# A hybrid decoder step: second score product over all rows, no GpSimd at the feed forward's entry, output projection in two halves

## The chip, the cores and the metric

One core of a Trainium2 chip runs the whole program: one layer over 1024 prompt tokens and 32 decode tokens (8 sequences of 4). The metric is the device time of one execution in microseconds (us). Engines are named as in the profile: PE (TensorE, with PEld for its weight loads), DVE (VectorE), ACT (ScalarE), POOL (GpSimd), SP (SyncE, which only issues DMAs here).

## The reference, cut to what matters

```
h  = rmsnorm(x, rms1_g) * (1 + sc1) + sh1                      # adaLN per sequence
z  = h @ w_in + b_in          # q, k, v, forget logits, glu_a, glu_b, gate_a, gate_b
s  = q @ k.T / 8 + C_q - C_k, causal;  p = softmax(s);  o = p @ v     # C = cumsum(logf)
y_a = o @ w_pa                                                 # attention branch
y_b = silu(layernorm(depthwise_conv(glu))) @ w_pb + b_pb       # convolution branch
m  = sigmoid(gate_a) * y_a + sigmoid(gate_b) * y_b
x  = x + g1 * (m @ w_o)                                        # output projection
h2 = rmsnorm(x, rms2_g) * (1 + sc2) + sh2
f_gate, f_up = split(h2 @ w_ffn_in)                            # 1024 -> 2 * 2816
x  = x + g2 * ((silu(f_gate) * f_up) @ w_ffn_out)
y  = rmsnorm(x, final_g)
```

D_MODEL is 1024, there are 8 heads of 64, and everything is float32. The 32 decode tokens attend to 1024 cached positions each.

## The kernel before, in words

Features lie on the 128 partitions and tokens along the free axis: the T = 1056 tokens (1024 prompt, 32 decode) are columns, and the 1024 features are KD = 8 tiles. A float32 product is made of three float32r products: an operand is split into a high part (an ACT cast, `wh`, L312) and the rest (a subtraction on DVE or POOL, `wl`, L315), and high times high, high times low and low times high are added up in PSUM (`mm3`, L324 to L326). `split_ahead` runs such a split at high priority, ahead of its turn.

The stages, in order of the code: input projection and the convolution; decode attention; prompt attention (`softmax_rows`, `load_head`, `scores`, `weighted`), with gate products and adaLN products (`gate`, `ada`) between; the two branches (`branch`, once for the convolution and once for attention); the output projection with `w_o`; the feed forward; its second projection with the last norm.

*Prompt attention.* A unit is a head and a pair of 128-row blocks. For each block `softmax_rows` makes scores in pieces of up to 512 columns in one PSUM tile `pss`: a first product of `q` and `k` over 128 rows (L813; the 64 upper rows hold one part of the split q, the 64 lower ones the other, and k's high part is there twice), a mask for the last piece (L815), and a second product over the 64 rows of `sl` alone, high q with low k (L816). Then DVE takes a minimum (L818), ACT an exponential (L824). `weighted` turns the probabilities (L871) and multiplies them with v (L883, L884). `load_head` brings a head in by seven DMAs, of which one is `kl` (L848).

*Branches.* `branch` goes over 8 row tiles and, in each, over three pieces of CW3 = 352 tokens. `out_a`, of the attention branch, adds the two gated branches on POOL (L965) and splits the sum into 48 pieces of 16 `rows` tiles (L966, L967), which are the inputs `merged` of the output projection.

*Output projection.* Three blocks `c` of 352 tokens. Each block loads and splits all eight tiles of `w_o`, multiplies (24 matmuls of 352 columns per tile), adds the residual (`residual`, L1051) and sums squares (L1066); `rstd` then makes 1/rms of the block with small DVE operations (L200 to L211) and spreads it over the partitions by diagonal tiles `dg` and a product with ones (L216, L217), and ACT copies it into `R` (L1090). After block 1 stands `half_factors(0)`.

*Feed forward.* It runs in halves `q` of SUP = 528 tokens, each of two quarters of HS = 264, by Winograd's form of Strassen's scheme: `half_factors(q)` makes seven split sums of the normed input (`u` L1011 and L1013, differences L1030, L1033, L1035, L1040, splits L1019 and L1020), `pair_weights` seven split sums of the weights (L1124, L1125, sums L1134, L1136, L1137, L1139), and `hidden_half` seven products of 12 matmuls with 264 columns (L1167): 84 matmuls per tile and half. Tiles 0 to 3 run for half 0 alone at first, tiles 4 to 21 for both, and tiles 0 to 3 for half 1 at the end. POOL takes part: the differences L1030 and L1033, two of the seven splits of `half_factors`, the weight sums of tiles 1 to 3 (not 0, `DV`), and four splits of `w_o` in block 2.

A scheduler with its own estimate of durations orders each engine's instructions; they then run in that order. Tile pools set when a buffer is free again.

The lines that choose engine and width before:

```
w = split_ahead(w_o[j], KD, pool if c == 2 and j % 2 else dve, *where)
w = pair_weights(t, dve if len(halves) == 2 or t in DV else pool)
```

Of the kernel before, what the change touches and what calls it, by code (L numbers as in the profile page):

```python
# [48 lines left out]
DV = (0,)  # L49
# [38 lines left out]
def hybrid_step(ctx, tc, xT, cT, vec, bvf, con, stT, ptab, ptabr, kcT, vc, lfc, w_ada, w_in, w_vfa, w_vfb,  # L88
# [97 lines left out]
    def rstd(s, n, denom):  # L186

        nb = -(-n // P)
        nf = n // P
        v = sm.tile([P, 4], F32, name="rv", tag="rv", bufs=2)  # L190
# [13 lines left out]
        y = sm.tile([P, 4], F32, name="ry", tag="ry", bufs=2)[:, :nb]  # L204
        t = sm.tile([P, 4], F32, name="rt", tag="rt", bufs=2)[:, :nb]
# [7 lines left out]
        pr = ps_st()  # L213
        for b in range(nb):
            m = min(P, n - b * P)
            dve.tensor_scalar(dg[:m, b * P:b * P + m], ident[:m, :m], y[:m, b:b + 1], None, OP.mult)  # L216
            pe.matmul(pr[:, b * P:b * P + m], ones[:m, :], dg[:m, b * P:b * P + m], start=True, stop=True)  # L217
        return pr
# [615 lines left out]
    def load_head(h):  # L834
# [111 lines left out]
    def branch(which, src, w_p, out):  # L946
        xs = split_act(src)
        for j in range(KD):
            w = split_ahead(w_p[j], 4, pool)
            for o in range(0, T, CW3):  # L950
                zg = ev(wp, "gev", 4)[:, :CW3]
                sp.dma_start(zg, gD[which][j][:, o:o + CW3])
                act.activation(zg, zg, AF.Sigmoid)
                ps = ps_mm()
                gemm(ps, w, lambda k: (xs[k][0][:, o:o + CW3], xs[k][1][:, o:o + CW3]), 4, CW3)
                out(j, o, ps[:, :CW3], zg)
# [5 lines left out]
    def out_a(j, o, ps, zg):  # L962
        h, l = [merged(o // CW3, r, j) for r in range(2)]
        dve.tensor_tensor(zg, ps, zg, OP.mult)
        (pool if j < KD - 1 else dve).tensor_tensor(zg, zg, X(j)[:, o:o + CW3], OP.add)  # L965
# [3 lines left out]
    branch(1, cvD, w_pb, out_b)  # L969
# [6 lines left out]
    def bp_tile(i, dt=F32R):  # L976
        return bp.tile([P, 3 * CW3], dt, name="b", tag=f"b{i}", bufs=1)
# [3 lines left out]
    def merged(c, r, j):  # L981
        i = (c * 2 + r) * KD + j
        return rows[i // 3][:, i % 3 * CW3:(i % 3 + 1) * CW3]

    branch(0, oD, w_pa, out_a)
# [7 lines left out]
    def half_factors(q, new):  # L993
# [66 lines left out]
    def sq_add(s, first, x, n, eng=dve):  # L1060
        if first:
            act.activation(s[:, :n], x, AF.Square)
        else:
            q = ev(sm, "sq", 2, (P, 400))
            act.activation(q[:, :n], x, AF.Square)
            eng.tensor_tensor(s[:, :n], s[:, :n], q[:, :n], OP.add)  # L1066

    for c in range(3):
        o = CW3 * c
        s = sm.tile([P, 400], F32, name="s1", tag="ssum", bufs=2)  # L1070
        for j in range(KD):
# [9 lines left out]
            ps = ps_mm()  # L1081
            gemm(ps, w, lambda k: (merged(c, 0, k), merged(c, 1, k)), KD, CW3)
            xj = X(j)[:, o:o + CW3]
            with tc.high_priority() if j == KD - 1 else nullcontext():
                residual(xj, ps, j, o, CW3, 16, xr)
                sq_add(s, j == 0, xj, CW3)
            sp.dma_start(xD[:, j, o:o + CW3], xj)
        with tc.high_priority():
            pr = rstd(s, CW3, D)
        act.copy(R[:, o:o + CW3], pr[:, :CW3])  # L1090
        if c == 1:
# [36 lines left out]
    def pair_weights(t, eng):  # L1128
# [270 lines left out]
```

## Time and profile before

| | |
|---|---|
| runs shown | 1669.34, 1672.14, 1674.14 us; median 1672.14 |
| profiled execution | 1673.01 us, its span 1671.2 us |
| PE busy | 1600.6 us, 96% of the span, 10988 matmuls |
| DVE, ACT, POOL busy | 1074.1 us (64%), 702.6 us (42%), 251.9 us (15%) |
| granted clock, mean | 0.98 of full speed |
| moved by DMA | 263.93 MB, mean 158 GB/s |

The span is what lies between the first and the last instruction of the trace; 1.8 us lie around it. PE is the busiest engine nearly everywhere, but its busy time counts a matmul from start to modelled end, with gaps of a pipeline inside it. So the distance from one matmul's start to the next one's is read beside it: the count of matmuls (x) in a stretch against its length.

### The profile page before, as it was taken

What the parts mean: (1) busy time and instruction counts of PE and PEld (TensorE: products, weight loads), DVE (VectorE), ACT (ScalarE), POOL (GpSimd) and SP (SyncE); (2) the same over time, 40 slices, a digit from 0 to 9 for tenths busy, and PEclk for the clock granted to TensorE, in tenths of its full rate; (3) what the DMA queues carried; (4) which work ended last, traced back from release to release, by engine and by line L of the source; (5) the groups of instructions that cost most, each with busy time, mean ns of one, the idle gap of its engine ahead of it and who ended that gap; (6) DMA issues with size and microseconds to landing.
All of it is one profiled execution on the core that took longest, in us unless ns stands there. A gap on an engine that the chain in (4) does not pass through costs nothing.

```text
span 1671.2 us, 29144 instructions
## 1 busy us (share of the span) xinstructions
PE 1600.6 (96%) x10988; PEld 1486.8 (89%) x10988; DVE 1074.1 (64%) x2119; ACT 702.6 (42%) x1395; POOL 251.9 (15%) x185
## 2 busy tenths in 40 slices
PE   6999999999999999999999789999999999999997
PEld 4999978788867777989998779999999999999997
DVE  6943389999787757234678995555555587324654
ACT  4552212122476555434554554333333365324442
POOL 2121113332220001125305430000000030000000
PEclk9999999999999979999999899999999999999998
DMA  9186576877486654354674322222222246424552
GB/s 363 62 285 185 159 226 176 249 234 224 150 247 211 185 166 145 114 187 123 211 219 156 102 85 101 77 77 77 77 82 83 80 155 214 157 87 146 172 184 84
DMA packets 143087, 263.93 MB, mean 158 GB/s; under 512 B 26810, under 2 KB 84794, under 8 KB 142306
## 3 DMA queue, kind: packets, MB, share of 16 engines
q1 hardware_dynamic: 104466, 211.46, 40.6%
q10 hardware_dynamic: 36384, 43.01, 7.4%
q0 software_dynamic: 2096, 7.60, 1.5%
q8 instruction: 86, 1.41, 0.4%
q14 instruction: 55, 0.45, 0.1%
HBM read 208.54 MB, written 53.48 MB: 157 GB/s over the span
## 4 chain that ended last, share of the span: by engine, by line
PE 70%; DVE 14%; DMA 7%; issue 3%; ACT 3%; SPq 2%; POOL 1%; ACTq 0%; DVEq 0%; POOLq 0%
PE mm L1167 23%; PE mm L1268 15%; DVE acc L525 7%; PE mm L326 6%; PE mm L324 6%; PE mm L325 6%; PE ptr L871 2%; PE pss L816 2%; DMA wa<-w_ada 1%; DMA gev<-gD 1%; PE ppv L884 1%; DVE wc L1125 1%; PE mm L162 1%; PE ppv L883 1%; PE pss L813 1%
## 5 line engine op out<-in xcount | busy, mean ns | idle before, releaser
L324 PE MATMUL mm<-ah,wh 128*128 128x384 f32 (+2 forms) x768 | 254.2, 332 | 7.4 <-ACT ah L288 3.6
L1268 PE MATMUL mm<-f,wo 128*128 128x352 f32 x1584 | 256.7, 323 | 0.0
L1268 PEld LDWEIGHTS mm<-f,wo 128*128 128x128 f32 x1584 | 254.7, 188 | 0.0
L326 PE MATMUL mm<-ah,wl 128*128 128x384 f32 (+2 forms) x768 | 253.0, 331 | 1.5 <-POOL wl L315 1.5
L325 PE MATMUL mm<-al,wh 128*128 128x384 f32 (+2 forms) x768 | 254.2, 331 | 0.0
L1167 PE MATMUL mm<-b,wc 128*128 128x264 f32 x1680 | 229.6, 288 | 10.3 <-ACT gev L1172 6.9
L1167 PE MATMUL mm<-c,wc 128*128 128x264 f32 x1776 | 235.5, 286 | 3.3 <-DVE gev L1189 3.3
L1167 PEld LDWEIGHTS mm<-c,wc 128*128 128x128 f32 x1776 | 225.2, 189 | 3.7 <-DVE gev L1189 3.7
L1167 PEld LDWEIGHTS mm<-b,wc 128*128 128x128 f32 x1680 | 217.0, 191 | 11.7 <-ACT gev L1172 7.3
L315 POOL TENSOR_TENSOR wl<-wr,wh 128x1024 fp32r<-128x1024 f32 (+1 forms) x48 | 122.1, 2547 | 440.3 <-ACT wh L312 417.3
L525 DVE SCALAR_TENSOR_TENSOR acc<-u,vec,acc 128x1024 f32<-128x1024 f32 x120 | 174.1, 1472 | 1.2
L324 PEld LDWEIGHTS mm<-ah,wh 128*128 128x128 f32 x768 | 146.5, 191 | 19.2 <-issue 7.9
L325 PEld LDWEIGHTS mm<-al,wh 128*128 128x128 f32 x768 | 146.6, 191 | 12.2 <-issue 11.7
L326 PEld LDWEIGHTS mm<-ah,wl 128*128 128x128 f32 x768 | 146.4, 191 | 7.6 <-issue 4.9
L1219 DVE TENSOR_TENSOR wo<-wr,wo 128x512 fp32r<-128x512 f32 x108 | 69.7, 647 | 129.7 <-ACT wo L1218 129.1
L1124 ACT CAST wc<-wr 128x512 fp32r<-128x512 f32 x144 | 88.0, 620 | 131.2 <-PE mm L1167 123.9
L1125 DVE TENSOR_TENSOR wc<-wr,wc 128x512 fp32r<-128x512 f32 x144 | 108.6, 760 | 37.1 <-ACT wc L1124 36.0
L1218 ACT CAST wo<-wr 128x512 fp32r<-128x512 f32 x108 | 63.2, 585 | 150.3 <-PE mm L1268 145.4
L312 ACT CAST wh<-wr 128x1024 fp32r<-128x1024 f32 (+1 forms) x72 | 68.1, 951 | 91.3 <-PE mm L325 71.9
L1134 POOL TENSOR_TENSOR s<-wr 128x512 f32<-128x512 f32 x6 | 13.1, 2188 | 400.6 <-DMA wr<-w_fi 387.1
L326 PE MATMUL mm<-yh,wl 128*128 128x352 f32 x192 | 61.9, 325 | 1.2 <-POOL wl L315 1.2
L324 PE MATMUL mm<-b,wh 128*128 128x352 f32 x192 | 62.1, 323 | 0.8 <-ACT wh L312 0.8
(299 smaller groups left out, 2731.6 us busy)
## 6 DMA issues: line engine op xcount, KB each, us to landing
wr<-w_fi SPq DMA_DIRECT2D x52, 512.0 KB
wa<-w_ada SPq DMA_DIRECT2D x48, 512.0 KB
wr<-w_fo SPq DMA_DIRECT2D x36, 512.0 KB
kt<-kcT SPq DMA_DIRECT2D x64, 256.0 KB
vt<-vc SPq DMA_DIRECT2D x64, 256.0 KB
wr<-w_o SPq DMA_DIRECT2D x24, 512.0 KB
hD<-h ACTq DMA_DIRECT2D x44, 264.0 KB
wr<-w_in SPq DMA_DIRECT2D x18, 512.0 KB
```

Source lines behind the costliest of these rows:

```text
L312: d = act.copy(wh[:, r, :], raw[:, r, :])
L315: eng.tensor_tensor(wl[:, r, :], raw[:, r, :], wh[:, r, :].bitcast(F32), OP.subtract)
L324: pe.matmul(ps[:, :n], wh[:, k, :], xh, start=(k == 0), stop=False)
L325: pe.matmul(ps[:, :n], wh[:, k, :], xl, start=False, stop=False)
L326: pe.matmul(ps[:, :n], wl[:, k, :], xh, start=False, stop=(k == nk - 1))
L525: dve.scalar_tensor_tensor(a[:, :NP], u[:, j:j + NP], wv[:, j:j + 1], a[:, :NP], op0=OP.mult, op1=OP.add)
L1124: act.copy(w[:, 0, :n], raw)
L1125: dve.tensor_tensor(w[:, 1, :n], raw, w[:, 0, :n].bitcast(F32), OP.subtract)
L1167: pe.matmul(ps[:, :HS], w[i][:, r, k * P:(k + 1) * P], x[s][:, k, :], start=(new and k == 0 and j == 0), stop=(k == 3 and j == 2), skip_gr ...
L1218: act.copy(x[:, 0, :], raw)
L1219: dve.tensor_tensor(x[:, 1, :], raw, x[:, 0, :].bitcast(F32), OP.subtract)
L1268: pe.matmul(ps[e][:, :n], w[r][:, k * P:(k + 1) * P], f[x], start=(k0 + k + i == 0), stop=(k0 + k == HT - 1 and i == 2))
```

## The change

1. **Attention.** The second score product runs over all 128 rows: `kl` now holds k's low part twice (two DMAs of 256 KB per head, not one), q's two parts have one fixed order, and the 64-row slice `sl` is gone. The product so also adds low q times low k.
2. **GpSimd.** In `half_factors`, `pair_weights` and the splits of `w_o` every operation that POOL had is DVE's.
3. **Output projection in halves.** The blocks of 352 tokens become two halves of 528, each of two pieces of 264 columns that share one load and one split of a `w_o` tile: 16 loads and splits, not 24. `half_factors(0)` stands after half 0. For it, `branch` for attention runs four pieces of 264, `rows` is laid out in pieces of 528, and `rstd` takes 528 tokens in five column groups (two PSUM tiles, three `dg` slots in turn).

```diff
-            pe.matmul(ps[:, :w], q[sl, qb], kl[sl, s0:s0 + w], start=False, stop=True)
+            pe.matmul(ps[:, :w], q[:, qb], kl[:, s0:s0 + w], start=False, stop=True)
...
         for r in range(2):
-            sp.dma_start(q[64 * r:64 * r + 64, :].bitcast(F32), qd[r ^ h2][sl, :])
-            sp.dma_start(k[64 * r:64 * r + 64, :].bitcast(F32), kd[0][sl, :])
-        sp.dma_start(kl[sl, :].bitcast(F32), kd[1][sl, :])
+            rows = slice(64 * r, 64 * r + 64)
+            sp.dma_start(q[rows, :].bitcast(F32), qd[r][sl, :])
+            sp.dma_start(k[rows, :].bitcast(F32), kd[0][sl, :])
+            sp.dma_start(kl[rows, :].bitcast(F32), kd[1][sl, :])
...
-    branch(0, oD, w_pa, out_a)
+    branch(0, oD, w_pa, HS, out_a)
...
         for k in ks:
-            pool.tensor_tensor(u11[:, k, :], u12[:, k, :], u11[:, k, :], OP.subtract)
+            dve.tensor_tensor(u11[:, k, :], u12[:, k, :], u11[:, k, :], OP.subtract)
             split_u(t1, k, u11)
         for k in ks:
-            pool.tensor_tensor(u12[:, k, :], u22[:, k, :], u12[:, k, :], OP.subtract)
-            split_u(b22, k, u22, pool)
+            dve.tensor_tensor(u12[:, k, :], u22[:, k, :], u12[:, k, :], OP.subtract)
+            split_u(b22, k, u22)
...
-    for c in range(3):
-        o = CW3 * c
-        s = sm.tile([P, 400], F32, name="s1", tag="ssum", bufs=2)
+    for q in range(2):
+        o = SUP * q
+        s = ev(lt2, "s1", 1, (P, SUP))
         for j in range(KD):
 
-            where = () if c == 0 and j < 2 else (lt2, ("wh3", "wl3"), 3)
-            w = split_ahead(w_o[j], KD, pool if c == 2 and j % 2 else dve, *where)
-            xr = ev(lt2, "xr", 3)
+            where = () if q == 0 and j < 2 else (lt2, ("wh3", "wl3"), 2)
+            w = split_ahead(w_o[j], KD, dve, *where)
+            xr = ev(lt2, "xr", 2, (P, SUP))
...
-            ps = ps_mm()
-            gemm(ps, w, lambda k: (merged(c, 0, k), merged(c, 1, k)), KD, CW3)
-            xj = X(j)[:, o:o + CW3]
+            pss = [ps_mm() for _ in range(2)]
+            for k in range(KD):
+                for i, ps in enumerate(pss):
+                    mm3(ps, w, k, KD, *[merged(q, r, k)[:, i * HS:(i + 1) * HS] for r in range(2)], HS)
+            xj = X(j)[:, o:o + SUP]
...
-        if c == 1:
+        if q == 0:
             B = [half_factors(0, lambda: by_four([bp_tile(i) for i in range(14)]))]
...
-            w = pair_weights(t, dve if len(halves) == 2 or t in DV else pool)
+            w = pair_weights(t)
```

What it does to the order of the instructions shows on DVE and on POOL. First DVE where the 1/rms of the first block of the output projection is done and `half_factors(0)` begins (`u<-XA` are its first operations, `XA<-mm` and `XB<-mm` the residuals of the output projection, `s<-s,sq` its sums of squares, `wl<-wr,wh` splits of `w_o`). Before:

```order
L216 TENSOR_SCALAR dg<-con,ry 128x128 x2
L216 TENSOR_SCALAR dg<-con,ry 96x96
L1051 SCALAR_TENSOR_TENSOR XA<-mm,mod,xr 128x352
L315 TENSOR_TENSOR wl<-wr,wh 128x1024
L1066 TENSOR_TENSOR s_10204<-s_10204,sq 128x352
L1011 SCALAR_TENSOR_TENSOR u<-XA,gP,R 128x264 x4
L1051 SCALAR_TENSOR_TENSOR XA<-mm,mod,xr 128x352
L1011 SCALAR_TENSOR_TENSOR u<-XB,gP,R 128x264 x4
L315 TENSOR_TENSOR wl<-wr,wh 128x1024
L1020 TENSOR_TENSOR b<-u,b 128x528
L1066 TENSOR_TENSOR s_10204<-s_10204,sq 128x352
L1051 SCALAR_TENSOR_TENSOR XB<-mm,mod,xr 128x352
```

And now, at the same place:

```order
L1054 SCALAR_TENSOR_TENSOR XA<-mm,mod,xr 128x264
L1054 SCALAR_TENSOR_TENSOR XA<-mm,mod,xr 128x232
L1058 TENSOR_TENSOR rs<-mm,mod 128x32
L1061 TENSOR_TENSOR XA<-xr,rs 128x32
L318 TENSOR_TENSOR wl<-wr,wh 128x1024
L219 TENSOR_SCALAR dg<-con,ry 128x128
L1069 TENSOR_TENSOR s_10682<-s_10682,s_10813 128x528
L219 TENSOR_SCALAR dg<-con,ry 16x16
L1014 SCALAR_TENSOR_TENSOR u<-XA,gP,R 128x264 x4
L1014 SCALAR_TENSOR_TENSOR u<-XB,gP,R 128x264 x4
L1014 SCALAR_TENSOR_TENSOR u<-XA,gP,R 128x264 x4
L1014 SCALAR_TENSOR_TENSOR u<-XB,gP,R 128x264 x4
```

Before, the first of `half_factors(0)` needs the first 352 tokens alone (the first `dg` rows) and the first two groups of four `u` stand between residuals of the second block; now five `dg` operations for 528 tokens come first (the last two are in these rows), and all sixteen `u` follow one another.

Next POOL, from its last part in the output projection to the end of the first `half_factors` (`u` and `b` are of `half_factors`, `s` and `wr` of `pair_weights`, `rv` is a fill in `rstd`). Before:

```order
L315 TENSOR_TENSOR wl<-wr,wh 128x1024 x2
L192 MEMSET rv 128x4
L315 TENSOR_TENSOR wl<-wr,wh 128x1024
L1030 TENSOR_TENSOR u<-u 128x528 x2
L1033 TENSOR_TENSOR u<-u 128x528 x2
L315 TENSOR_TENSOR wl<-wr,wh 128x1024
L1020 TENSOR_TENSOR b<-u,b 128x528 x4
L1134 TENSOR_TENSOR s_11150<-wr 128x512
L1136 TENSOR_TENSOR wr<-wr 128x512
L1137 TENSOR_TENSOR wr<-s_11150,wr 128x512
L1139 TENSOR_TENSOR wr<-wr 128x512
```

And now, the last that POOL does in the program:

```order
L318 TENSOR_TENSOR wl<-wr,wh 128x512
L968 TENSOR_TENSOR gev<-gev,XB 128x264 x3
L318 TENSOR_TENSOR wl<-wr,wh 128x512
L968 TENSOR_TENSOR gev<-gev,XB 128x264 x5
L192 MEMSET rv 128x5 x3
```

POOL's last tensor operation is now one of `out_a`; behind it are only fills.

Last DVE in the feed forward's first tiles, where a set of weights is made while a tile is multiplied (`wc` and `b` are splits of weights, `gev` and `h` operations of `hidden_half`, `rt` and `ry` of the last `rstd` of the output projection). Now:

```order
L1144 TENSOR_TENSOR s_11549<-wr 128x512
L209 TENSOR_TENSOR rt<-ry 128x5
L1146 TENSOR_TENSOR wr<-wr 128x512
L210 SCALAR_TENSOR_TENSOR rt<-rt,rv 128x5
L1135 TENSOR_TENSOR b<-s_11549,b 128x512
L1147 TENSOR_TENSOR wr<-s_11549,wr 128x512
L211 SCALAR_TENSOR_TENSOR ry<-rt,ry 128x5
L1196 TENSOR_TENSOR gev<-gev,mm 128x264
L1135 TENSOR_TENSOR wc<-wr,wc 128x512
L1149 TENSOR_TENSOR wr<-wr 128x512
L209 TENSOR_TENSOR rt<-ry 128x5
L1199 TENSOR_TENSOR gev<-gev,mm 128x264
```

The four sums of a tile's weights (two write `wr` from `wr` alone, one writes `s`, one reads it) stand among the splits on DVE; before they stood on POOL for tiles 1 to 3, as in the rows of POOL above.

## Rows read from the trace of the kernel before

**Rows 1.** The page: the chain that ended last.

```profile
PE 70%; DVE 14%; DMA 7%; issue 3%; ACT 3%; SPq 2%; POOL 1%; ACTq 0%; DVEq 0%; POOLq 0%
```

**Rows 2.** Windows by stage: busy us of each engine (x instructions), PE clock, DMA.

```profile
410.00:680.00 270.00, 265.33 (x1658) 208.34 (x1657) 193.85 (x574) 153.92 (x312) 37.84 (x29) 0.97 0.60 181
440.00:540.00 100.00, 98.53 (x639) 74.39 (x637) 82.02 (x266) 65.59 (x133) 14.19 (x15) 1.00 0.64 195
...
1340.00:1400.00 60.00, 56.74 (x444) 56.32 (x444) 47.50 (x83) 35.11 (x79) 14.70 (x10) 0.97 0.50 158
...
862.90:1010.10 147.20, 126.51 (x874) 123.94 (x874) 133.99 (x234) 81.24 (x163) 57.26 (x34) 0.93 0.39 124
...
820.00:840.00 20.00, 20.00 (x126) 19.84 (x126) 13.03 (x19) 8.51 (x13) 0.00 (x0) 1.00 0.85 269
...
1200.00:1220.00 20.00, 20.00 (x166) 20.00 (x165) 10.52 (x21) 7.42 (x17) 0.00 (x0) 1.00 0.23 80
```

**Rows 3.** Line L816: durations ns min/median/max, forms; idle before it.

```profile
L816 PEld LDWEIGHTS pss<-kl,q x96: 182/183/285, 410.8 to 670.7; 64*128 64x128 f32 x96
L816 PE MATMUL pss<-kl,q x96: 323/491/792, 410.8 to 670.7; 64*128 64x512 f32 x48, 64*128 64x384 f32 x16, 64*128 64x128 f32 x16, 64*128 64x256 f32 x16
...
  issue: 11.7, 47
```

**Rows 4.** Timeline of PE around score products: start, length, instruction.

```profile
430.96 0.40 PE L813 MATMUL pss<-k,q 128*128 128x512 f32 x1
431.29 0.50 PE L816 MATMUL pss<-kl,q 64*128 64x512 f32 x1
431.72 0.44 PE L324 MATMUL mm<-ah,wh 128*128 128x384 f32 x1
432.00 0.34 PE L325 MATMUL mm<-al,wh 128*128 128x384 f32 x1
432.17 0.39 PE L813 MATMUL pss<-k,q 128*128 128x512 f32 x1
432.40 0.22 PE L815 MATMUL pss<-maskr,identr 128*128 128x128 f32 x1
...
500.23 0.32 PE L816 MATMUL pss<-kl,q 64*128 64x128 f32 x1
500.49 0.44 PE L324 MATMUL mm<-ah,wh 128*128 128x384 f32 x1
```

**Rows 5.** DVE timeline: first work of `half_factors(0)`.

```profile
862.91 1.71 DVE L1011 SCALAR_TENSOR_TENSOR u<-XA,gP,R 128x264 f32<-128x264 f32 x4 [1.54 <-ACT R L1090]
```

**Rows 6.** DVE groups, 862.9 to 1010.1 us: busy us, mean ns, idle before.

```profile
L1125 DVE TENSOR_TENSOR wc<-wr,wc 128x512 fp32r<-128x512 f32 x25 | 23.8, 962 | 1.0 <-ACT wc L1124 1.0
L1066 DVE TENSOR_TENSOR s<-s,sq 128x352 f32<-128x352 f32 x12 | 10.7, 890 | 1.2 <-ACT sq L1065 1.2
L1125 DVE TENSOR_TENSOR b<-wr,b 128x512 fp32r<-128x512 f32 x10 | 9.4, 953 | 0.7 <-ACT b L1124 0.7
L1020 DVE TENSOR_TENSOR b<-u,b 128x528 fp32r<-128x528 f32 x10 | 8.0, 807 | 0.0
...
L1011 DVE SCALAR_TENSOR_TENSOR u<-XB,gP,R 128x264 f32<-128x264 f32 x12 | 7.2, 664 | 0.0
L1011 DVE SCALAR_TENSOR_TENSOR u<-XA,gP,R 128x264 f32<-128x264 f32 x12 | 5.1, 488 | 1.9 <-ACT R L1090 1.9
L1125 DVE TENSOR_TENSOR wc<-s,wc 128x512 fp32r<-128x512 f32 x4 | 4.8, 1198 | 0.1
L1190 DVE TENSOR_TENSOR h<-gev 128x264 f32<-128x264 f32 x6 | 4.7, 789 | 0.1
```

**Rows 7.** The same groups of DVE in the steady part, 1020 to 1340 us.

```profile
L1125 DVE TENSOR_TENSOR wc<-wr,wc 128x512 fp32r<-128x512 f32 x95 | 66.2, 699 | 33.6 <-ACT wc L1124 32.6
...
L1190 DVE TENSOR_TENSOR h<-gev 128x264 f32<-128x264 f32 x31 | 13.4, 434 | 3.0 <-ACT wc L1124 0.4
```

**Rows 8.** POOL groups, 862.9 to 1010.1 us.

```profile
L1020 POOL TENSOR_TENSOR b<-u,b 128x528 fp32r<-128x528 f32 x4 | 6.1, 1540 | 6.5 <-ACT b L1019 6.5
```

More of the change, by code (lines that the diff above doesn't have):

```diff
@@ L189, in rstd @@
         nf = n // P
-        v = sm.tile([P, 4], F32, name="rv", tag="rv", bufs=2)
+        v = sm.tile([P, 5], F32, name="rv", tag="rv", bufs=2)
         if n % P:
@@ L212, in rstd @@
         dg = sm.tile([P, 400], F32, name="dg", tag="dg", bufs=1)
-        pr = ps_st()
+        prs = []
         for b in range(nb):
             m = min(P, n - b * P)
-            dve.tensor_scalar(dg[:m, b * P:b * P + m], ident[:m, :m], y[:m, b:b + 1], None, OP.mult)
-            pe.matmul(pr[:, b * P:b * P + m], ones[:m, :], dg[:m, b * P:b * P + m], start=True, stop=True)
-        return pr
+            if b % 4 == 0:
+                prs.append(ps_st())
+            d, to = b % 3 * P, b % 4 * P
+            dve.tensor_scalar(dg[:m, d:d + m], ident[:m, :m], y[:m, b:b + 1], None, OP.mult)
+            pe.matmul(prs[-1][:, to:to + m], ones[:m, :], dg[:m, d:d + m], start=True, stop=True)
+        return prs if n > 512 else prs[0]
     def sumsq(tiles, n, eng=dve):
@@ L944, in split_act, with branch @@
         return r
-    def branch(which, src, w_p, out):
+    def branch(which, src, w_p, width, out):
         xs = split_act(src)
@@ L949, in branch @@
             w = split_ahead(w_p[j], 4, pool)
-            for o in range(0, T, CW3):
-                zg = ev(wp, "gev", 4)[:, :CW3]
-                sp.dma_start(zg, gD[which][j][:, o:o + CW3])
+            for o in range(0, T, width):
+                zg = ev(wp, "gev", 4)[:, :width]
+                sp.dma_start(zg, gD[which][j][:, o:o + width])
                 act.activation(zg, zg, AF.Sigmoid)
                 ps = ps_mm()
-                gemm(ps, w, lambda k: (xs[k][0][:, o:o + CW3], xs[k][1][:, o:o + CW3]), 4, CW3)
-                out(j, o, ps[:, :CW3], zg)
+                gemm(ps, w, lambda k: (xs[k][0][:, o:o + width], xs[k][1][:, o:o + width]), 4, width)
+                out(j, o, ps[:, :width], zg)
     def out_b(j, o, ps, zg):
@@ L962, in out_a @@
     def out_a(j, o, ps, zg):
-        h, l = [merged(o // CW3, r, j) for r in range(2)]
+        h, l = [merged(o // SUP, r, j)[:, o % SUP:o % SUP + HS] for r in range(2)]
         dve.tensor_tensor(zg, ps, zg, OP.mult)
-        (pool if j < KD - 1 else dve).tensor_tensor(zg, zg, X(j)[:, o:o + CW3], OP.add)
+        (pool if j < KD - 1 else dve).tensor_tensor(zg, zg, X(j)[:, o:o + HS], OP.add)
         act.copy(h, zg)
         dve.tensor_tensor(l, zg, h.bitcast(F32), OP.subtract)
-    branch(1, cvD, w_pb, out_b)
+    branch(1, cvD, w_pb, CW3, out_b)
     gate(7, pool, sp)
@@ L976, in bp_tile, with merged @@
     def bp_tile(i, dt=F32R):
-        return bp.tile([P, 3 * CW3], dt, name="b", tag=f"b{i}", bufs=1)
+        return bp.tile([P, T], dt, name="b", tag=f"b{i}", bufs=1)
     rows = [bp_tile(i) for i in range(16)]
-    def merged(c, r, j):
-        i = (c * 2 + r) * KD + j
-        return rows[i // 3][:, i % 3 * CW3:(i % 3 + 1) * CW3]
-    branch(0, oD, w_pa, out_a)
+    def merged(q, r, j):
+        i = (q * 2 + r) * KD + j
+        return rows[i // 2][:, i % 2 * SUP:(i % 2 + 1) * SUP]
+    branch(0, oD, w_pa, HS, out_a)
     ykp.release()
@@ L1058, in residual, with sq_add @@
             dve.tensor_tensor(dst[:, npr:n], src[:, npr:n], t, OP.add)
-    def sq_add(s, first, x, n, eng=dve):
+    def sq_add(s, first, x, n, q=None):
         if first:
@@ L1080, in hybrid_step @@
                     sp.dma_start(xr[:, lo - o:hi - o], xT[:, at + lo:at + hi])
[L1081 to L1091 removed]
+            pss = [ps_mm() for _ in range(2)]
[3 more added lines that the diff above has]
+            xj = X(j)[:, o:o + SUP]
+            with tc.high_priority() if j == KD - 1 else nullcontext():
+                for i, ps in enumerate(pss):
+                    part = slice(i * HS, (i + 1) * HS)
+                    residual(xj[:, part], ps, j, o + i * HS, HS, 16, xr[:, part])
+                sq_add(s, j == 0, xj, SUP, ev(lt2, "s2", 2, (P, SUP)) if j else None)
+            sp.dma_start(xD[:, j, o:o + SUP], xj)
+        with tc.high_priority():
+            prs = rstd(s, SUP, D)
+        for i, pr in enumerate(prs):
+            n = min(512, SUP - 512 * i)
+            act.copy(R[:, o + 512 * i:o + 512 * i + n], pr[:, :n])
+        if q == 0:
             B = [half_factors(0, lambda: by_four([bp_tile(i) for i in range(14)]))]
```

28 lines of the change are left out of this document (13 added, 15 removed).

## The prediction

> **What bounds the kernel now.** I read the page's chain first, then windows by stage, then the timeline of PE inside a stage. The chain ends in PE for 70% and in DVE for 14% [rows 1]; so a microsecond of PE time counts in most stages, and the windows must show where it doesn't. In the steady feed forward PE starts 166 matmuls of 264 columns in 20 us, one per 120.5 ns; in the output projection 126 of 352 columns, one per 158.7 ns, both at the full granted clock (1.00, 2.4 GHz) [rows 2]. Against these two measures two stages are slow. In prompt attention (410 to 680 us) PE counts as busy for 265 of 270 us, DVE for 194, ACT for 154 [rows 2]: PE-bound, with holes inside the busy time, see below. From 862.9 us, when `half_factors(0)` begins [rows 5], to 1010.1 us, when the sixth product of tile and half is done, DVE is busy for 134.0 of 147.2 us [rows 2], and PE has 874 matmuls: some 274 of 352 and 600 of 264 columns, worth 43.5 + 72.3 = 116 us by the pitches above. There DVE sets the pace and PE loses 31 us.
>
> **Part 1, second score product.** It has 96 matmuls, all over 64 rows: 48 of 512 columns, 16 each of 384, 256 and 128 [rows 3]. In the timeline a first product of 512 columns over 128 rows, followed by another product over 128 rows, takes 0.23 us to the next start (432.17 to 432.40). Followed by L816 it takes 0.33 (430.96 to 431.29); L816 itself takes 0.43 (to 431.72), and the product behind it, of 384 columns, 0.28 (to 432.00), though the next of that width takes 0.17 (to 432.17) [rows 4]. So a 64-row product costs 0.10 + 0.20 + 0.11 = 0.41 us more than its columns. The narrowest, of 128 columns, takes 0.26 us to the next start (500.23 to 500.49) [rows 4], against about 0.11 by its columns: 0.15 instead of the 0.20. Behind a mask product, 64 of the 96 times, the loss ahead is nearer 0.04 (64 pieces are last pieces; the 32 others carry 0.10 to 0.18). That gives 32 x 0.45 + 64 x 0.33 = 14 + 21 = 35 us of PE time. An idle row of 11.7 us before its weight loads, put down to "issue" [rows 3], is the visible third of it.
>
> The Trainium skill (TensorEngine Tiling (Array Packing), Key Properties) says that changing the tiling mode drains the engine; the rows above are what that looks like here, with the loss on both sides of the product. The Trainium skill (TensorE: Matmul & The Clock Gate, Part 3) also speaks against the edit: small products in different row groups run beside each other, which a product over all rows gives up. Each L816 of the rows stands alone between 128-row products, so by that rule nothing is lost here.
>
> What takes the place of the 35 us? Without it the stage would be 235 us; DVE's 194 us would fill 83% of it, in its first part (440 to 540 us: 82 of 100 us [rows 2], shrinking to some 87) 94%. There waits for the softmax will eat part. Added are 8 DMAs of 256 KB, 2.1 MB at the stage's 181 GB/s: 12 us beside a DMA share of 0.60 [rows 2], hidden unless a head comes late. Bounds: 35 us gained at most, nothing if DVE and DMA hold the pace. I take 28, four fifths, because DVE is near its limit in a third of the stage only.
>
> **Part 2, narrower pieces.** The output projection goes from 576 matmuls of 352 columns (91.4 us) to 768 of 264 (92.5 us), the attention branch from 288 (45.7) to 384 (46.3): +1.7 us by the two pitches [rows 2], and I set it against 8 splits and loads of `w_o` fewer, which lie under PE. ACT and POOL do the same elements in 32 pieces, not 24, under a PE that is busy throughout (93.2 of 94 us, 814 to 908 us [rows 2], for the projection).
>
> **Part 3, POOL's work on DVE, and the halves.** What POOL costs DVE today: a subtraction of 512 columns takes DVE 699 ns in the steady part, without POOL [rows 7], and 962, 953 and 1198 ns in the entry [rows 6]. L1190 takes 434 against 789 [rows 6, 7], `u` from XA 488 and from XB 664 [rows 6]. Times their counts: 25 x 0.263 + 10 x 0.254 + 4 x 0.499 + 6 x 0.355 + 12 x 0.176 = 6.6 + 2.5 + 2.0 + 2.1 + 2.1 = 15.3 us. L1066 by the same measure (352 of 512 columns, about 0.52) adds 12 x 0.37 = 4.4 and L1020's 20 at 0.807 against 0.72 another 1.7. This is 21 us; a dozen smaller groups of that answer add up to some 12 by the same subtraction. The floor is 21, the ceiling POOL's own 57 us [rows 2]; I take 33.
>
> The Trainium skill (SBUF — State Buffer, Who interferes with whom) says that a VectorE instruction with two SBUF inputs and a GpSimd instruction that reads SBUF lock each other out for a whole instruction. The doubled durations agree. By that rule a wait can be as long as POOL's instruction, here 1.5 us [rows 8].
>
> What DVE takes over until the sixth product: by the order, 16 operations of 528 columns and 14 of 512, 16 x 0.72 + 14 x 0.70 = 21 us alone, 18 back to back. It loses two splits of 1024 columns (2.5), one `rstd` chain (2.5) and 2 us of smaller sums. That leaves +11. So its 134 us become 134 - 33 + 11 = 112, and its 13 us of idle time some 8: 120 us.
>
> But it starts later. Before, the first `u` came 48.5 us after the output projection's first product (814.4 to 862.9 [rows 2, 5]), on the first 352 tokens. Now the fourth `dg` stands behind 516 of 768 matmuls and the fifth behind 521: about 63 us, and with the projection's first waits and ACT's copy 66. Until then DVE has little to do. The sixth product so ends 66 + 120 = 186 us after the projection's start, against 195.7: 10 us gained. The bounds: if the long durations had another cause than POOL, 66 + 134 + 11 + 8 = 219, 23 us lost; if DVE no longer held PE up, PE's lost 31 us come back.
>
> At the end, tiles 1 to 3 of half 1 move the same way (PE busy 56.7 of 60 us, POOL 14.7 [rows 2]); 12 sums at 0.7 are 8.4 us for DVE against about as much blocking. I take 1 us gained, between 3 lost and 3 gained.
>
> **Sum.** 1673.0 us of the profiled execution - 28 - 10 + 0 - 1 = 1634; the median of the runs shown is 0.9 lower, so 1633 on its scale.
>
> **Rivals.**
> *Attention turns into a wait.* PE reaches its score products earlier and waits for DVE, or for a head's load, which grows by a ninth. For it: DVE's 82 of 100 us. Against: gate products stand between the score products (L324) [rows 4] and wait for neither. It would give 10, not 28: 1651.
> *The entry loses.* DVE takes POOL's work and starts 18 us later, and the long durations stay in part. For it: DVE is the bound there and gets more work. Against: the steady rows of the same forms. At 12 us lost: 1673 - 28 + 12 - 1 = 1656.
> *Both give all.* 35 in attention, 25 at the entry, 3 late: 1610.
> *The second product isn't sped up.* The wait behind it may belong to the weight load, not to its 64 rows: 1673 - 10 - 1 = 1662. Against it: the load of a 128-row product starts no gap of this kind.
> *Slower: weight loads show under 264 columns.* Each matmul loads its own weights, also where two pieces share them, and a load lasts longer than 264 columns stream. A load of 128 columns lasts 183 ns [rows 3]. If each matmul of 264 columns in the projection and the branch took that long, 1152 x 0.183 - 864 x 0.159 = 211 - 137 = +74 us, where the sum has +2: 1634 + 72 = 1706. It decides from 1152 x (p - 0.1205) = 39, that is p = 154 ns. The trace speaks against it with 120.5 ns for 264 columns with a weight load each. The Trainium skill (TensorE: Matmul & The Clock Gate, Part 3) has the rule that could make it so, that loads overlap running products only in other row groups; the feed forward's pitch disagrees with it.
>
> **How the numbers follow.** The forecast, 1633, has 0.55 and its own range 1618 to 1646; attention as a wait 0.17, a losing entry 0.12, both in full 0.10, the second product unchanged 0.03, slower 0.03. Leaving out the slow one and a little of each end, the range is 1609 to 1660. A difference under 0.3%, 5 us, can't be told from none here. Faster holds the forecast, the full gain and nearly all of the next two: 0.91; 0.05 for no change, from the ends of the entry and the unchanged product; 0.04 slower.
>
> **What would show it.** Right for attention: L816's successor follows a 512-column product after 0.23 us, the 128-row product behind it is not stretched, the idle time by "issue" is gone, and 410 to 680 us shrinks by 20 to 35. Right for the entry: DVE's 512-column subtraction near 0.70 us there, first `u` some 66 us after the first product of the projection, more matmuls per 20 us behind it. The output projection and the branch keep 120 ns per matmul. Wrong would be waits of PE on `px`, `st` or `wa` that grow by as much as the drains were, or a sixth product later than 196 us after the projection's start.

## The result and the profile after

The changed kernel takes 1632.49 us (median of four runs, 1629.86 to 1636.82), the kernel before 1672.95 in the same job: a ratio of 0.9764 (95% interval 0.9734 to 0.9795), or 34 to 45 us less. The forecast was 1633. The profiled execution has 1629.88 us, 43.1 less than that of before. That its end and the forecast meet hides errors of opposite sign, which the experiments show.

The page of the changed kernel: the granted clock in 40 slices, and the chain that ended last, which answers to [rows 1].

```profile
PEclk9999999999999999999999999999999999999998
...
PE 72%; DVE 12%; DMA 7%; ACT 3%; issue 3%; POOL 2%; SPq 1%; ACTq 0%; DVEq 0%; POOLq 0%
```

Read it stage by stage: the page's shares hardly move. First the windows of the kernel before from its first to its last score product, and from the output projection's first product to the end of the twelfth product of tile and half (columns as in [rows 2]):

```profile
410.40:670.40 260.00, 255.34 (x1588) 198.54 (x1586) 189.56 (x563) 148.51 (x302) 35.46 (x28) 0.97 0.62 186
...
814.40:1069.90 255.50, 234.04 (x1664) 230.72 (x1663) 200.87 (x356) 125.72 (x245) 57.36 (x35) 0.96 0.43 138
```

The same two stretches of the kernel after, then the parts that the prediction spoke of: the score stage from 440 to 540 us, the output projection at work, the steady feed forward, and from the first `u` to the sixth product of tile and half.

```profile
410.50:645.20 234.70, 222.26 (x1586) 191.02 (x1585) 187.08 (x560) 149.28 (x302) 34.64 (x28) 0.99 0.73 215
...
790.30:1030.40 240.10, 231.89 (x1861) 228.32 (x1862) 179.40 (x376) 118.28 (x235) 0.55 (x3) 0.99 0.39 130
...
440.00:540.00 100.00, 94.27 (x691) 78.47 (x690) 86.87 (x289) 74.94 (x154) 18.36 (x18) 1.00 0.76 221
840.00:860.00 20.00, 20.00 (x166) 19.80 (x166) 11.98 (x37) 6.06 (x9) 0.10 (x1) 1.00 0.51 162
1200.00:1220.00 20.00, 20.00 (x166) 20.00 (x165) 10.65 (x21) 7.88 (x17) 0.00 (x0) 1.00 0.24 81
...
858.70:973.30 114.60, 108.67 (x854) 105.92 (x855) 109.43 (x237) 74.82 (x153) 0.10 (x1) 0.99 0.34 116
```

The score stage is 25.3 us shorter with the same counts of instructions (to within three), the second stretch 15.4 us shorter with more of them: DVE has 20 more and is busy for 21.5 us less. The last 3 us come in the tiles at the end: from the 40th to the 44th product of tile and half it took 43.7 us, now 40.2.

Not all of the 25.3 us belong to the edit. In both traces the granted clock falls to its lower level, 1.2 GHz, at one place of the score stage, while PE waits for a DMA of `wa`, weights of an adaLN product (2.6 us before, 2.5 now). Before, it stayed there for 17.0 us, now for 6.8:

```profile
593.10:610.10 17.00, 15.83 (x56) 11.80 (x57) 6.10 (x26) 8.50 (x19) 2.36 (x1) 0.50 0.51 138
...
577.90:584.70 6.80, 5.73 (x30) 3.47 (x31) 1.84 (x8) 2.54 (x7) 0.00 (x0) 0.50 0.60 219
```

At half the speed the 10.2 us more cost some 5 us: an estimate, half of them, since PE is the bound there. The last section holds it against three executions of the same code.

The timeline of PE around score products (answers to [rows 4]): L815 is the first product, L817 the mask, L818 the second product.

```profile
430.40 0.40 PE L815 MATMUL pss<-k,q 128*128 128x512 f32 x1
430.64 0.39 PE L818 MATMUL pss<-kl,q 128*128 128x512 f32 x1
430.87 0.33 PE L327 MATMUL mm<-ah,wh 128*128 128x384 f32 x1
431.04 0.34 PE L328 MATMUL mm<-al,wh 128*128 128x384 f32 x1
431.21 0.39 PE L815 MATMUL pss<-k,q 128*128 128x512 f32 x1
431.44 0.22 PE L817 MATMUL pss<-maskr,identr 128*128 128x128 f32 x1
431.50 0.44 PE L818 MATMUL pss<-kl,q 128*128 128x512 f32 x1
```

L818 starts 0.24 us after L815, its successor 0.23 us after it and the one behind 0.17 us later. Before these were 0.33, 0.43 and 0.28. So where no mask stands before it, no stretch is left on either side of the second product. Behind a mask one stays, on L818 itself: 0.29 us (431.50 to 431.79) for the same 512 columns. The line of the second product has lost its idle row of 11.7 us by "issue" (answers to [rows 3]); what is left ahead of its weight loads is one short wait:

```profile
L818 PEld LDWEIGHTS pss<-kl,q x96: 186/188/333, 410.7 to 645.8; 128*128 128x128 f32 x96
...
its engine sat idle before it (us, times) until:
  DMA kl<-qkD: 0.2, 1
```

The first `u` on DVE's timeline (answers to [rows 5]), 68.4 us after the start of the projection at 790.3:

```profile
858.74 1.70 DVE L1014 SCALAR_TENSOR_TENSOR u<-XA,gP,R 128x264 f32<-128x264 f32 x4 [2.70 <-ACT R L1100]
```

DVE's groups from the first `u` to the sixth product (answers to [rows 6]):

```profile
L1135 DVE TENSOR_TENSOR wc<-wr,wc 128x512 fp32r<-128x512 f32 x25 | 16.9, 690 | 0.8 <-ACT wc L1134 0.8
...
L1023 DVE TENSOR_TENSOR b<-u,b 128x528 fp32r<-128x528 f32 x14 | 9.5, 704 | 0.0
L1135 DVE TENSOR_TENSOR b<-wr,b 128x512 fp32r<-128x512 f32 x10 | 6.8, 687 | 0.0
...
L1014 DVE SCALAR_TENSOR_TENSOR u<-XB,gP,R 128x264 f32<-128x264 f32 x12 | 5.2, 487 | 0.0
...
L1069 DVE TENSOR_TENSOR s<-s,s 128x528 f32<-128x528 f32 x6 | 4.2, 704 | 0.0
...
L1196 DVE TENSOR_TENSOR gev<-gev,mm 128x264 f32<-128x264 f32 x6 | 2.6, 432 | 0.0
...
L1200 DVE TENSOR_TENSOR h<-gev 128x264 f32<-128x264 f32 x6 | 2.6, 428 | 0.0
```

Every group of this list that was long in [rows 6] is shorter: 690 from 962, 687 from 953, 704 from 807, 487 from 664, 428 from 789 ns; L1069 takes 704 ns for 528 columns where 352 took 890. The two of them that [rows 7] shows in the steady part, at 699 and 434 ns, are back there. The one group above that has an input in PSUM (`gev<-gev,mm`) was never long. The kernel before, in the same stretch as [rows 6], beside POOL:

```profile
L1189 DVE TENSOR_TENSOR gev<-gev,mm 128x264 f32<-128x264 f32 x6 | 2.5, 421 | 1.1 <-PE mm L1167 0.9
```

Where POOL stood in [rows 8] only a fill of 0.1 us is left.

### The profile page after: what moved, and what is told of

Read it like the earlier page. It is cut to its first block, busy times and chain, and to the rows that moved or that the text cites. A ratio compares the mean times of both kernels' runs of the same rounds, so it can differ in the third digit from the quotient of the medians.

```text
span 1628.1 us, 29682 instructions
## 1 busy us (share of the span) xinstructions
PE 1564.1 (96%) x11280; PEld 1475.9 (91%) x11280; DVE 1048.5 (64%) x2161; ACT 697.3 (43%) x1398; POOL 178.2 (11%) x147
## 4 chain that ended last, share of the span: by engine, by line
PE 72%; DVE 12%; DMA 7%; ACT 3%; issue 3%; POOL 2%; SPq 1%; ACTq 0%; DVEq 0%; POOLq 0%
PE mm L1177 25%; PE mm L1278 16%; PE mm L329 7%; PE mm L328 7%; PE mm L327 7%; DVE acc L528 4%; DMA wa<-w_ada 2%; DMA gev<-gD 2%; POOL wl L318 1%; PE ptr L874 1%; PE mm L561 1%; PE mm L560 1%; PE mm L562 1%; DMA sq<-hD 1%; PE ppv L887 1%
## 5 line engine op out<-in xcount | busy, mean ns | idle before, releaser
L327 PE MATMUL mm<-ah,wh 128*128 128x384 f32 (+2 forms) x768 | 252.9, 330 | 8.8 <-ACT gev L384 4.0
L329 PE MATMUL mm<-ah,wl 128*128 128x384 f32 (+2 forms) x768 | 251.5, 329 | 2.2 <-POOL wl L318 2.2
L318 POOL TENSOR_TENSOR wl<-wr,wh 128x1024 fp32r<-128x1024 f32 (+1 forms) x44 | 111.8, 2545 | 396.0 <-ACT wh L315 340.9
L1135 DVE TENSOR_TENSOR wc<-wr,wc 128x512 fp32r<-128x512 f32 x144 | 98.5, 689 | 36.0 <-ACT wc L1134 35.0
L315 ACT CAST wh<-wr 128x1024 fp32r<-128x1024 f32 (+1 forms) x64 | 59.7, 939 | 93.1 <-PE mm L328 56.6
L329 PE MATMUL mm<-b,wl 128*128 128x264 f32 x256 | 72.3, 286 | 2.2 <-DVE wl L318 2.2
L327 PE MATMUL mm<-b,wh 128*128 128x264 f32 x256 | 72.9, 285 | 1.3 <-ACT wh L315 1.3
```

The lines of the kernel that those rows point to most:

```text
L315: d = act.copy(wh[:, r, :], raw[:, r, :])
L318: eng.tensor_tensor(wl[:, r, :], raw[:, r, :], wh[:, r, :].bitcast(F32), OP.subtract)
L327: pe.matmul(ps[:, :n], wh[:, k, :], xh, start=(k == 0), stop=False)
L329: pe.matmul(ps[:, :n], wl[:, k, :], xh, start=False, stop=(k == nk - 1))
L1135: dve.tensor_tensor(w[:, 1, :n], raw, w[:, 0, :n].bitcast(F32), OP.subtract)
```

## The experiments

Each run was timed beside the kernel before on its chip (its median was 1666.48 us for the three parts alone and the mask product, 1665.67 for the other four). "Entry" below is the stretch from the output projection's first product to the twelfth product of tile and half: 255.5 us before, 240.1 after.

### Second score product alone

Only the edits of part 1, from the list of the change.

```diff
-            pe.matmul(ps[:, :w], q[sl, qb], kl[sl, s0:s0 + w], start=False, stop=True)
+            pe.matmul(ps[:, :w], q[:, qb], kl[:, s0:s0 + w], start=False, stop=True)
```

> The kernel before with part 1 of the change alone (second score product over all 128 rows, kl loaded twice). Theory A (the three parts add up, and each acts in its own stage): attention shortens by the 25 us that separate the two traces at the last score product; the last score product starts near 645 us, the feed forward's entry stays as it was (sixth product of tile and half some 196 us after the output projection's first), total 1672 - 25 = 1647 us, 1643 to 1652. Theory B (the gain in attention needs the later parts, or the shift of the stages behind it changes them): more than 5 us away from that.

Measured: 1648.56 us, ratio 0.9908 (0.9873 to 0.9942), 10 to 21 us gained. The score stage has 234.3 us, the entry 254.5, as before, so the part acts in its own stage, as theory A has it. Its 25 us are not confirmed: the time falls into 1643 to 1652 us only because the kernel before ran faster here than the 1672 that the range starts from, and as a gain 25 lies above the interval.

### DVE in POOL's place, alone

```diff
-            split_u(b22, k, u22, pool)
+            split_u(b22, k, u22)
...
-            w = split_ahead(w_o[j], KD, pool if c == 2 and j % 2 else dve, *where)
+            w = split_ahead(w_o[j], KD, dve, *where)
```

and the same for the other operations of part 2.

> The kernel before with part 2 alone: half_factors, pair_weights and w_o splits have no operation on POOL. Theory A (POOL's reads held DVE up): DVE's 512-column subtraction takes 0.69 us in the entry, not 0.96; DVE's busy time from first u to sixth product falls from 134 by 33 and rises by some 20 of moved work, and the sixth product comes 10 to 15 us earlier: total 1656 to 1662 us. Theory C (the halves make the gain at the entry, POOL's work is only moved): 0 to 4 us, 1668 to 1673.

Measured: 1655.81 us, ratio 0.9936 (0.9912 to 0.9960), 7 to 15 us gained. The entry in its windows:

```profile
812.20:1055.20 243.00, 232.50 (x1665) 230.46 (x1664) 186.91 (x385) 125.13 (x242) 0.30 (x3) 0.96 0.44 143
```

DVE does 29 instructions more than before in this stretch and is busy for 14.0 us less; the entry is 12.5 us shorter. DVE's 512-column subtraction (`wc<-wr,wc`) takes 685 ns in it, and the sixth product comes 13.3 us earlier. That is theory A: the gain at the entry is here without the halves.

### The halves alone

The loop over two halves and the layout of `rows`, with POOL's operations left where they were.

```diff
-    for c in range(3):
-        o = CW3 * c
+    for q in range(2):
+        o = SUP * q
```

> The kernel before with part 3 alone: output projection in two halves, branch in pieces of 264, POOL keeps its operations (sums of tiles 1 to 3, two differences and two splits of half_factors, and in the second half every second split of w_o). Theory A: no gain, since first u comes 18 us later while DVE is nearly idle and POOL then blocks DVE as before; sixth product 0 to 10 us later, total 1672 to 1684. Theory C (the halves make the gain): 10 to 15 us faster, 1657 to 1662. 264-column matmuls keep 0.1205 us each in both.

Measured: 1673.12 us, ratio 1.0045 (1.0019 to 1.0070): 3 to 12 us slower. The entry takes 259.2 us, 3.7 more than before, and the two branches ahead of it 114.9 against 110.3. DVE's 512-column subtractions stay long, 819 (`wc<-wr,wc`) and 1066 ns (`b<-wr,b`). Theory A again; theory C is out. The score stage, whose code is the kernel's before, took 252.9 us here against 260.0.

### Parts 1 and 2 without the halves

The changed kernel with the output projection in three blocks of 352 tokens again.

```diff
-    for q in range(2):
-        o = SUP * q
+    for c in range(3):
+        o = CW3 * c
```

> Parts 1 and 2 together, the output projection left in three blocks of 352 tokens. Theory A (the parts add up, and the gain at the entry is GpSimd's share of it; the halves alone gave no gain, 1.0045 of the time before): within 4 us of the changed kernel, 1630 to 1637 us on the scale of its runs, 0.974 to 0.979 of the time before; first product of the output projection to the twelfth product of tile and half about 243 us, as with part 2 alone. Rival B (the halves, which alone were hurt by GpSimd's splits of w_o, are worth their part once GpSimd is gone): 5 to 10 us slower than the changed kernel, 1637 to 1643.

Measured: 1630.62 us, ratio 0.9792 (0.9763 to 0.9820). The changed kernel has 0.9764 (0.9734 to 0.9795): no difference that can be told. Between theory A and rival B that does not decide: on the scale of the changed kernel's runs 0.9792 is 1638 us, in rival B's range, and the interval, 1633 to 1643, reaches into both. By the ends of the two intervals the halves may lose 5 us or win 14.

The traces say where to look. The entry takes 243.2 us, as in the run of part 2 alone (243.0); with the halves it took 240.1, and 242.4 in the next run, which has the same code there. So the halves give 1 to 3 us, and the clock may be part of that: PE stood at 1.2 GHz for 13.7 us of the 243.2 and for 3.4 of the 240.1. The two branches took 111.3 us with the halves against 108.7 in this run; over all runs (but the halves alone) they took 109.5 to 111.4 with pieces of 264, 110.8 in the mean, and 108.6 to 110.4 with 352, 109.5 in the mean, so some 1.3 us go there.

### One score product of three back on 64 rows

In the changed kernel the mask product sums over its first 64 rows alone.

```diff
-                pe.matmul(ps[:, w - P:w], identr, maskr, start=False, stop=False)
+                pe.matmul(ps[:, w - P:w], identr[:64, :], maskr[:64, :], start=False, stop=False)
```

> The changed kernel with the mask product over 64 rows, not 128, so that only the first 64 rows of the mask count (it leaves out half of the causal mask). The product has the same 128 columns and weights. Theory D (a change between a 64-row and a 128-row product stops PE, whatever the products): 64 mask products cost some 0.1 us ahead, 0.15 themselves and 0.1 behind, 64 x 0.35 = 22 us of PE time; attention lengthens by 15 to 22 us, total 1648 to 1655. Theory E (the loss was the length or the weights of the second product itself): no change, 1632.

Measured: 1642.08 us, ratio 0.9847 (0.9815 to 0.9880). Its score stage, and PE's timeline at one mask product:

```profile
408.00:662.40 254.40, 245.15 (x1586) 200.24 (x1584) 186.39 (x560) 150.50 (x303) 35.24 (x28) 0.97 0.68 198
```

```profile
433.01 0.33 PE L815 MATMUL pss<-k,q 128*128 128x384 f32 x1
433.28 0.32 PE L817 MATMUL pss<-maskr,identr 64*128 64x128 f32 x1
433.53 0.44 PE L818 MATMUL pss<-kl,q 128*128 128x384 f32 x1
433.81 0.29 PE L328 MATMUL mm<-al,wh 128*128 128x288 f32 x1
```

The same piece in the changed kernel:

```profile
434.43 0.33 PE L815 MATMUL pss<-k,q 128*128 128x384 f32 x1
434.60 0.22 PE L817 MATMUL pss<-maskr,identr 128*128 128x128 f32 x1
434.65 0.39 PE L818 MATMUL pss<-kl,q 128*128 128x384 f32 x1
434.88 0.29 PE L328 MATMUL mm<-al,wh 128*128 128x288 f32 x1
```

A product of half as many rows makes the stage 19.7 us longer, and PE busy for 22.9 us more. Ahead of it the 384 columns take 0.27 us to the next start instead of 0.17, the mask itself 0.25 instead of 0.05, the product behind it 0.28 instead of 0.23. That is 0.10 + 0.20 + 0.05 = 0.35 us, 22 us for 64 of them: a loss ahead, on the product and behind it, as the prediction read from [rows 4], but with a smaller last part, because here the product behind a full mask is stretched too. The edit changes nothing but the count of rows, so the count of rows is the cause, theory D; whether in the load or in the product isn't shown. Of the 19.7 us the clock has some 3 (an estimate, half of the difference: 13.6 us at 1.2 GHz here, 6.8 in the changed kernel). The profiled execution is the slowest of the four, and the two ratios, 0.9847 and 0.9764, are 14 us apart.

### POOL reading beside DVE

The changed kernel, with two subtractions by POOL of a part of `u` from itself at each split, into a tile that nothing reads.

```diff
             act.copy(b[0][:, k, :], u[:, k, :])
+            x = uq.tile([P, 1, HS], F32, name="sc", tag="sc", bufs=1)
+            for i in range(k.start, k.stop):
+                pool.tensor_tensor(x, u[:, i:i + 1, :], u[:, i:i + 1, :], OP.subtract)
```

> The changed kernel with GpSimd subtracting a part of u from itself into a scratch tile that nothing reads, two operations of 264 columns beside each of the 14 splits of the seven sums (about 1.6 us each time, some 23 us of GpSimd in the entry, as much again in the second half). Theory (GpSimd's reads of SBUF stop DVE's operations with two SBUF inputs for as long as they last): DVE's 512-column subtraction behind the first u goes from 690 to over 800 ns, the entry grows by 5 to 12 us. Rival (DVE's long durations had another cause, such as its own queue or ACT): no more than 2 us.

Measured: 1649.59 us, ratio 0.9904 (0.9871 to 0.9937). The entry takes 257.4 us, 17.3 more than after. In its windows, and in DVE's groups from the first `u` to the sixth product:

```profile
791.70:1049.10 257.40, 236.64 (x1860) 233.18 (x1859) 197.93 (x375) 119.43 (x234) 60.20 (x59) 0.97 0.37 122
```

```profile
L1138 DVE TENSOR_TENSOR wc<-wr,wc 128x512 fp32r<-128x512 f32 x25 | 18.5, 749 | 0.0
L1026 DVE TENSOR_TENSOR c<-u,c 128x528 fp32r<-128x528 f32 x14 | 11.9, 880 | 0.0
...
L1014 DVE SCALAR_TENSOR_TENSOR u<-XB,gP,R 128x264 f32<-128x264 f32 x12 | 7.0, 639 | 0.0
...
L1203 DVE TENSOR_TENSOR h<-gev 128x264 f32<-128x264 f32 x6 | 3.4, 568 | 0.1
...
L1199 DVE TENSOR_TENSOR gev<-gev,mm 128x264 f32<-128x264 f32 x6 | 2.5, 420 | 0.4 <-PE mm L1180 0.4
```

DVE is busy for 18.5 us more than after with one instruction less. The last two rows are the telling pair: same engine, operation, size and time; the one with both inputs in SBUF (`h<-gev`) goes from 428 to 568 ns, the one with an input in PSUM (`gev<-gev,mm`) stays (432 after, 420 here). The subtraction of 512 columns was expected over 800 ns: `b<-wr,b` reached 805, the more frequent `wc<-wr,wc` 749. The time grew more than expected; PE was at 1.2 GHz for 17 us of the stretch, not 3.4, which may be part of that.

### POOL writing beside DVE

As above, but POOL copies one column of `u` and then fills the tile six times.

```diff
+            pool.tensor_copy(x[:, 0, 0:1], u[:, k.start, 0:1])
+            for _ in range(6):
+                pool.memset(x, 0.0)
```

> As the run with GpSimd's reads, but GpSimd copies one column of u and then fills the scratch tile six times (264 columns each, about as long in all) without reading. Theory (it is the reads that stop DVE): the 512-column subtraction stays near 700 ns and the entry within 2 us of the changed kernel's. Rival (any GpSimd work on SBUF stops DVE): the same growth as with the reads, 5 to 12 us.

Measured: 1635.94 us, ratio 0.9817 (0.9781 to 0.9852). The entry in its windows, and the same group of DVE:

```profile
792.10:1039.60 247.50, 234.01 (x1858) 230.68 (x1859) 180.06 (x376) 117.96 (x235) 81.58 (x199) 0.98 0.38 126
```

```profile
L1027 DVE TENSOR_TENSOR c<-u,c 128x528 fp32r<-128x528 f32 x14 | 9.5, 700 | 0.0
```

POOL is busy for 81.6 us, more than with the reads, and DVE's time stays: 180.06 against 179.40 us for as many instructions. So it is the reads that stretch DVE's operations. The time was expected within 2 us and missed: the entry is 7.4 us longer than after. Not by DVE's durations; PE is busy for 2.1 us more, at a lower clock, and idle for 5.3 us more, its longest wait 4.7 us for ACT's `wc`. ACT in turn waits there 3.7 us for a load of weights (`wr<-w_fi`), which it doesn't in the changed kernel; why that load came late isn't shown. The lower clock, 10.2 us at 1.2 GHz and not 3.4, has at most some 3 us of the 7.4. By the timed runs the two kernels can't be told apart: the intervals overlap.

### Four splits of `w_o` kept for the second half

```diff
-            w = split_ahead(w_o[j], KD, dve, *where)
+            w = held.pop(j) if j in held else split_ahead(w_o[j], KD, dve, *where)
+            if q == 0 and j in (0, 1, 6, 7):
+                held[j] = w
```

> The changed kernel, but four of the eight split tiles of w_o are kept from the first half and used again in the second, which takes tiles 6 and 7 first; DVE and ACT lose four splits of 1024 columns at the time when they make the first u. Theory: DVE's entry, 109 of 115 us busy behind the first u, gets 4 x 1.25 = 5 us less work: 2 to 5 us faster than the changed kernel. Rival (the four splits lie before the first u, where DVE has time): no difference over 2 us.

Measured: 1628.76 us, ratio 0.9777 (0.9748 to 0.9806), the changed kernel's within the interval. DVE is busy for 174.97 us of the entry, 4.4 less than after, and the entry takes 239.9 us against 240.1: the rival's figure was right, its reason by half. Ahead of the first `u`, where DVE has time, it was busy for 2.6 us less; between there and the sixth product, where it is busy for 95% of the time, for 2.1 us less, and that stretch became 0.9 us shorter. So a microsecond of DVE taken there is no longer one of the whole.

## Why the prediction was right

**Second score product: right in mechanism, too large in size.** The drains were read from four starts in the timeline, the changed kernel gives the same 0.10, 0.20 and 0.11 us back, and the mask test takes 0.10, 0.20 and 0.05 again. PE's busy time in the stage fell by 33.1 us (255.34 to 222.26), some 5 of it by the clock (17.0 and 6.8 us at 1.2 GHz), where 35 was worked out. But PE now waits: the stage less PE's busy time is 12.4 us where it was 4.7. PE's waits in the score stage after (before, `wa` had 3.3 us and no other over 0.8):

```profile
PE mm L161 <- DMA wa<-w_ada: 5.6, 5, 2.5
PE ptr L874 <- DVE ptl L877: 2.7, 3, 2.1
PE pst L780 <- DVE lnsum L778: 1.6, 1, 1.6
PE mm L327 <- DVE mod L173: 1.3, 1, 1.3
```

The rival "attention turns into a wait" so came true for 8 us; the sign of it that the prediction named, waits on `px`, `st` or `wa` as large as the drains, did not come, `wa` grew by 2.3 us. In the profiled pair 25 us remain, but that is a high value: without the edit the stage took 260.0, 258.1 and 252.9 us in three executions, with it 234.7, 234.3, 235.7, 239.0, 238.2 and 238.1. The means, 257.0 and 236.7, give 20 us, and the timed run of the edit alone 10 to 21. The term of 28 was mis-sized, by about 8; "four fifths" rested on one profile of before, whose score stage is the longest of the three, with the clock low for longest. Less half of its time at 1.2 GHz the stage has 251.2 to 251.5 us without the edit and 230.6 to 233.9 with it: 19 us for the edit, in six profiles against three. DVE's share from 440 to 540 us came out as worked out, 87 of 100 us.

**Narrower pieces: right.** 166 matmuls in 20 us in the projection, 120.5 ns each, each with its own weight load: the slower rival, which needed 154 ns, is out.

**Entry: right, and too small.** First `u` 68.4 us after the projection's first product (66 forecast), sixth product after 182.9 (186 forecast, 195.7 before); DVE busy for 109.4 of the 114.6 us between (112 of 120 forecast). So 12.8 us gained by then, 15.4 by the twelfth product, where the sum had 10. The 33 us taken for what POOL cost DVE come out in the run of part 2 alone: DVE busy for 14.0 us less with 29 operations more, some 20 us at 0.7 each, is 34. The durations that the prediction calls doubled are 1.1 to 1.8 times as long by its own rows. PE's loss there was read a little low: the trace has 290 matmuls of 352 and 560 of 264 columns in the 147.2 us, worth 113.5 us by the same pitches, not 116. And it wasn't DVE's pace alone: PE stood at 1.2 GHz for 20.4 of those 147.2 us, and for 3.4 of the 114.6 after the change; before each fall it had waited for a split of weights (2.7 us for ACT's `b`, 0.7 and 0.9 for DVE's `wc`). That is at most 10 of the 34 us lost (an estimate, half of the 20.4), and the prediction has no term for it. The rival "the entry loses" rested on long durations with another cause; POOL's reads are shown to be the cause by the runs with reads and with writes. The Trainium skill (SBUF — State Buffer, Who interferes with whom) names just these: DVE with two inputs from SBUF and a GpSimd that reads; the pair of 568 and 420 ns agrees. What failed is the credit for the halves: they were forecast as part of this term, and alone they lost. What they give at the entry once POOL is gone, 1 to 3 us, the branches take back in part, 1.3 us, where 0.6 was forecast for them; the timed runs show no gain. The runs don't show why the halves cost 3 to 12 us while POOL still reads.

**Late tiles: right in sign.** 3.5 us instead of 1, just past the bound of 3. DVE has 11 instructions more there (54 to 65) and is busy for 1.0 us less (33.6 to 32.5).

**The sum.** Timed apart, part 1 gives 15 (10 to 21) and part 2 11 (7 to 15) us; both together 35 (30 to 40). The ends of the two added up (16 to 36) overlap with that from 30 to 36; whether the two help each other isn't settled. The clock may be what they share: its mean over the runs is 0.982 or 0.983 in the kernel before and 0.982 with either part alone, but 0.987 with both and 0.9885 in the changed kernel. If PE were the bound throughout, 0.005 would be some 8 us, about the 9 by which both exceed the sum; no run holds the clock fixed, so this isn't shown. On the profiled executions the errors, attention 3 too high, the branches' 1.0 us left out, the entry and late tiles 8 too low, make 1630 of 1634. The forecast has no term for the clock, which is 0.980 and 0.992 in the profiled pair; the agreement of the medians is partly luck.

## What to carry to other kernels

Read the cost of a lone product of fewer rows from starts, not from its own duration: with its neighbours it took 0.35 us more than the same product over all rows, though its own row grew by 0.10 (0.22 to 0.32). Before work goes to POOL to relieve DVE, compare DVE's durations beside POOL's reads with the same forms elsewhere: here 57 us of POOL's work cost DVE more time than doing it. Look at the clock of a stage in both traces before its difference is put down to the edit. Time each part alone, since one of the three gave no gain that could be told.

## What the runs showed of the hardware

POOL's read waits for DVE too. In the run with POOL's writes the copy of a single column, the one operation that reads, has these durations (minimum, median, maximum in ns):

```profile
L1023 POOL COPY sc<-u x28: 185/665/4795, 863.7 to 972.9; 128x1 f32<-128x1 f32 x28
```

The longest, and the rows of DVE around its end (POOL's spans are rough):

```profile
902.50 4.79 POOL L1023 COPY sc<-u 128x1 f32<-128x1 f32 x1
...
906.57 0.69 DVE L1139 TENSOR_TENSOR wc<-s,wc 128x512 fp32r<-128x512 f32 x1
907.17 0.15 DVE L200 TENSOR_SCALAR rv<-pst 128x4 f32<-128x4 f32 x1
```

From 902.29 to 907.25 us DVE ran eight operations with two inputs in SBUF, one behind the other; POOL's copy of one column ended at 907.29, just after DVE had come to an operation that reads PSUM. So here POOL waited for more than one of DVE's operations.

The clock makes unchanged code differ. With the code of the kernel before, the score stage took 260.0, 258.1 and 252.9 us in three profiled executions (of that kernel and of the runs of part 2 and of the halves alone). In each PE waited 2.0 to 2.6 us for the same DMA of `wa`, and around that wait the clock fell to 1.2 GHz. It stayed there for 17.0, 13.6 and 3.4 us (windows of the last two):

```profile
594.00:607.60 13.60, 13.60 (x45) 10.38 (x44) 5.66 (x24) 6.83 (x15) 2.36 (x1) 0.50 0.50 129
...
590.60:594.00 3.40, 3.40 (x15) 3.06 (x14) 1.66 (x6) 1.83 (x4) 2.36 (x1) 0.50 0.38 136
```

Less half of that time the three are 251.5, 251.3 and 251.2 us. Why the same wait was followed by so different a time at the lower level isn't shown. The 7 us between them are more than half of what part 2 is worth; a part of that size is told by timed rounds, not by one pair of profiles.
